# Layer 0's first five modulations as narrow fp32 products on TensorE, and four stages in a new written order

## The chip, the cores and the metric

One core of a Trainium2 chip runs the whole program once. The metric is device time in microseconds (us) of one launch. Instructions run on TensorE (PE in the profile, its weight loads PEld), VectorE (DVE), ScalarE (ACT), GpSimd (POOL) and SyncE (SP, which here only issues DMAs). Matrix products read from SBUF and write to PSUM, which has eight banks here called ps4 to ps7 and psl0 to psl3.

## The reference

One step of a four-layer backbone over 512 latent and 128 context tokens with 1024 features. In front of each half-layer stands a modulated norm, whose shift, scale and gate come from a linear map of a conditioning vector; there are two such vectors, `c` for latents and `c_ctx` for context tokens:

```python
def ada_mod(cond, w, b):
    m = jax.nn.silu(cond) @ w + b              # w: 1024 x 6144, one per layer
    return jnp.split(m[..., None, :], 6, axis=-1)

for i in range(DEPTH):                         # mixers A, B, C, A
    sh, sc, gt, sh2, sc2, gt2 = ada_mod(cond, w_ada[i], b_ada[i])   # for c and for c_ctx
    h = rmsnorm(x, norm_g[i, 0]) * (1 + sc) + sh
    x = x + gt * mixer(h)                      # attention, then its output projection
    h = rmsnorm(x, norm_g[i, 1]) * (1 + sc2) + sh2
    x = x + gt2 * (jnp.square(jax.nn.relu(h @ w_in)) @ w_out)
```

All is float32. The six parts are called modulation 0 (shift) to 5 (second gate) below.

## The kernel before

**Layout.** Activations lie with features on the 128 partitions (eight feature tiles, ft) and 640 tokens along the free axis, in two halves of 320. A product in float32 precision is made of three products of parts: each operand is split in a high part (ScalarE copies it to `fp32r`) and a low part (VectorE takes the difference), and high x high, high x low and low x high are added up in one bank. So one unit (128 output features) on one half is 24 products of 320 columns. In the trace the weights' parts are `wa`, the normed activations' `ex` and `ar`. Weights come as units of 512 KB through two `wraw` buffers on SyncE's queue.

**The modulations of layer 0 before the change.** A column of 128 outputs is a tile of 128 x 1024 of the transposed weights (512 KB). `ada_tile` loads it and takes a row-wise product with the conditioning vector that was copied to all partitions (`cb`): on VectorE as one multiply-and-reduce (`junk<-adaw,cb` or `junk<-wa,cb`), or, for the second vector of the tiles marked `mix`, as a multiply on GpSimd (`adaw<-adaw,cb`, `wa<-wa,cb`) and a summing pass on ScalarE. Layer 0 needs modulations 0 and 1 before anything else can start, 2 to 4 by its output projection and second norm. Four tiles of modulation 0 (`SPE`) are products on TensorE instead: the weights are the stationary operand, the two conditioning vectors a moving operand of two columns. `cb` itself is made on TensorE from a table (`sel`) in `start`.

**Stages of layer 0.** `start`: loads, modulations 0 and 1, the first half's norm (`norm_ft`: `nt<-x,mod,ps`, then `ex` or `ar` on ScalarE and `ar<-nt,...` on VectorE) and products of four ready units feature tile by feature tile as the norm goes on. `mixer_ac`, order "0 qkv": the second half's norm and products of the four units, and the values (five token blocks, 24 products of 256 columns each), with the tiles of modulations 2 and 3 as steps in between. Order "0 qkv2": two key units and four more query units, both halves, 12 x 24 products. "0 attn": attention. "0 oproj": eight units of the output projection, which also add to the residual and to the sum of squares (`acc`), the second norm, and the first eight units of the MLP; with the rest of modulations 3 and 4 as steps, modulation 5 and layer 1's behind them. On this stage `ws.slow` sends every second low part of the weights to GpSimd (`wa<-wraw,wa` on POOL).

**What sets the order.** In these five stages the calls are collected and replayed in an order written out by hand as a table of numbers (`ORDER`), which then is each engine's program order, in `start` SyncE's too. Outside them a scheduler orders. Each engine executes in order, so an instruction that waits holds all behind it.

Of the kernel before, what the change touches and what calls it, by code (L numbers as in the profile page):

```python
# [12 lines left out]
F32 = mybir.dt.float32  # L13
F32R = mybir.dt.float32r
# [4 lines left out]
P = 128  # L19
D = 1024  # L20
# [7 lines left out]
SPE = 4  # L28
SMIX = ((5, 7), (1, 3, 5, 7))
SX = {0: 5, 1: 6}  # L30
SJ = (0, 0, 2, 4, 5, 6)
# [3 lines left out]
A0S = 29  # L35
# [10 lines left out]
ORDER = {  # L46
    "0 attn": """
# [19 lines left out]
    """,  # L67
    "0 oproj": """
# [10 lines left out]
    """,  # L79
    "0 qkv": """  # L80
# [5 lines left out]
    """,  # L86
    "0 qkv2": """
# [4 lines left out]
    """,  # L92
    "0 start": """
# [710 lines left out]
class Kern:  # L804
# [289 lines left out]
    def mixer_ac(self, l):  # L1094
# [6 lines left out]
        with ExitStack() as lc:  # L1101
            if l == 0:
                aw = self.renew(self.walloc(3), F32)
                self.adaw = Ring(aw)
                steps = self.ada_tiles(0, range(16, A0S), True)
# [10 lines left out]
            with tc.tile_pool(name=f"qkv{l}", bufs=2) as tp:  # L1116
# [103 lines left out]
                if l == 0:  # L1220
                    values()
                    for _ in steps:
                        pass
                    oc.close()
                    self.wfree(self.renew(aw, F32R))
                    oc.enter_context(self.ordered(f"{l} qkv2"))
# [32 lines left out]
        def oproj():  # L1259
            step = None  # L1260
            if l == 0:
                steps = self.ada_tiles(0, range(A0S, 40), True)
                step = lambda: [next(steps, None) for _ in range(4)]
            self.run_units(8, [o[0] for o in O], [o[1] for o in O],
                           lambda ps, f, half: self.x_update(ps, f, half, m[2], True),
                           ret_last=lambda: self.norm_begin(l, 1), step=step)
            for o in O:
                self.free(o)
# [157 lines left out]
    def mlp(self, l, oproj):  # L1426

        nc = self.nc
        with self.tc.tile_pool(name=f"mlp{l}", bufs=1) as mp:
# [7 lines left out]
            self.ws.slow = (2, 6, 0, 0)[l]  # L1437
# [64 lines left out]
    def ada_tile(self, l, k, i, mix=False, dma=None):  # L1502

        nc = self.nc
        m = self.mods[l][k]
        w = self.adaw()
        (dma or (nc.sync if mix else nc.gpsimd)).dma_start(w, self.a["ada"][l, 8 * k + i])
        for cond in (0, 1):
            c = self.cb[:, cond, :]
            if cond and mix:  # L1510
                nc.gpsimd.tensor_tensor(out=w, in0=w, in1=c, op=ALU.mult)
                nc.scalar.activation(w, w, AF.Copy, accum_out=m[:, cond, i:i + 1])
            else:
                with self.tc.issue_after(self.last.ins) if self.last else nullcontext():
                    j = self.junk
                    nc.vector.tensor_tensor_reduce(out=j, in0=w, in1=c, op0=ALU.mult, op1=ALU.add, scale=1.0, scalar=0.0, accum_out=m[:, cond, i:i + 1])
        if i == 7 and (l or k > 1):
            self.mod_done(l, k)

    def ada_tiles(self, l, fs, mix=False):  # L1520
        for f in fs:
            self.ada_tile(l, f // 8, f % 8, mix)
            yield

    def silu(self, c, mp, n):
# [5 lines left out]
        nc.vector.tensor_tensor(out=c, in0=c, in1=e, op=ALU.mult)  # L1531

    def start(self):

        nc, a = self.nc, self.a
        with self.tc.tile_pool(name="start", bufs=6) as mp:
            self.adaw = self.ring(mp, "adaw", D, 6)
# [3 lines left out]
            wt = self.renew(self.alloc(12), F32)  # L1541
            oc = ExitStack()
            oc.enter_context(self.ordered("0 start", True))
            nc.sync.dma_start(c1, a["cc"])
            nc.sync.dma_start(c2, a["cc2"])
            for i in range(4):
                nc.sync.dma_start(wt[i][:16, :512], a["sel"][i // 2][:, i % 2 * 512:i % 2 * 512 + 512])
            self.silu(c1, mp, "e16")
            self.silu(c2, mp, "e8")
            own, self.banks = self.banks[:NQ[0]], self.banks[NQ[0]:]  # L1550
            for i in range(4):
                pb = self.bank()
                for j in range(4):
                    nc.tensor.matmul(pb[:, j * P:j * P + P], wt[i][:16, j * P:j * P + P], c1, start=True, stop=True)
                nc.scalar.activation(self.cb.rearrange("p c d -> p (c d)")[:, i * 512:i * 512 + 512], pb, AF.Copy)
            self.mods_open(0)
            m, b = self.mods[0], self.mods[0][6]
            ps = self.bank()
# [18 lines left out]
            for ft in range(NF):  # L1577
# [4 lines left out]
                if ft == 0:  # L1582
                    load_x(0, 0)
# [174 lines left out]
```

## Time and profile before

| | |
|---|---|
| median of 3 runs (lowest, highest) | 3115.05 us (3114.43, 3116.70) |
| the profiled execution, its own time | 3113.05 us |
| its span, first to last instruction | 3111.2 us |
| TensorE busy | 2981.5 us, 96% of the span, 20016 products |
| VectorE, ScalarE, GpSimd busy | 2232.6 (72%), 1373.2 (44%), 668.0 us (21%) |
| mean granted TensorE clock | 0.983 of full speed |

TensorE's share of nearly the whole span says that the kernel as a whole is bound by products; the stages before and after layer 0's attention are where it is not, and the profile is read there by stages. A busy TensorE need not run at its peak: the granted clock has two levels, 2.4 GHz (1.00) and 1.2 GHz (0.50), and a window's number is the mean over it.

### The profile page before, as it was taken

The page shows a single profiled execution, that of the slowest core. Times are in us where ns is not written, and L with a number is a line of the kernel's source. Part 1 is how long each engine was busy: PE and PEld are TensorE (multiplying, and loading weights), DVE is VectorE, ACT ScalarE, POOL GpSimd, SP SyncE. Part 2 cuts the span into 40 slices and gives each one's busy share as a digit, 9 for nine tenths or more (in the row PEclk, how much of TensorE's full clock was granted, in tenths as well). Part 3 has the DMA queues.
Part 4 walks back from the last instruction along what each step waited for, and adds up shares of the span by engine and source line. Part 5 has one row for each costly group of instructions (what it writes and reads, how often), then busy time and mean ns, then how long its engine had stood idle before and what let it go on. Part 6 is the DMA issues. An engine that isn't in the chain of part 4 may idle for free. (4 is left out here: it accounts for less than half of the span.)

```text
span 3111.2 us, 52045 instructions
## 1 busy us (share of the span) xinstructions
PE 2981.5 (96%) x20016; PEld 2916.1 (94%) x20016; DVE 2232.6 (72%) x4697; ACT 1373.2 (44%) x2895; POOL 668.0 (21%) x760
## 2 busy tenths in 40 slices
PE   6789899999999999999998899999999999999998
PEld 6789899999989989999998889999999899999998
DVE  8998987677679779667559997766756896633444
ACT  3477433223368664223237793332233494422321
POOL 4556420000034351000003571000000270000000
PEclk8799999999999999999999999999999999999999
DMA  6302444443212124444321004344422102222221
GB/s 220 107 25 75 142 155 145 150 153 126 65 39 58 50 87 146 150 149 149 97 80 35 23 1 151 121 151 150 148 85 75 45 1 69 95 75 75 75 75 48
DMA packets 89305, 300.84 MB, mean 97 GB/s; under 512 B 11104, under 2 KB 15920, under 8 KB 88672
## 3 DMA queue, kind: packets, MB, share of 16 engines
q1 hardware_dynamic: 64816, 210.35, 21.0%
q0 software_dynamic: 24240, 87.16, 8.8%
q8 instruction: 157, 2.57, 0.4%
q14 instruction: 92, 0.75, 0.1%
HBM read 288.66 MB, written 3.56 MB: 94 GB/s over the span
## 5 line engine op out<-in xcount | busy, mean ns | idle before, releaser
L283 PE MATMUL ps<-ar,wa 128*128 128x320 f32 x6752 | 1151.2, 312 | 22.5 <-DVE ar L283 15.3
L283 PE MATMUL psl<-ar,wa 128*128 128x320 f32 x6392 | 1088.8, 311 | 9.9 <-ACT ar L283 3.7
L283 PEld LDWEIGHTS ps<-ar,wa 128*128 128x128 f32 x6752 | 1038.2, 189 | 29.4 <-DVE ar L283 19.7
L283 PEld LDWEIGHTS psl<-ar,wa 128*128 128x128 f32 x6392 | 982.5, 189 | 12.9 <-ACT ar L283 4.1
L283 ACT ACTIVATE wa<-wraw 128x1024 fp32r<-128x1024 f32 (+3 forms) x350 | 359.9, 1030 | 938.4 <-PE psl L283 438.2
L283 DVE TENSOR_TENSOR wa<-wraw,wa 128x1024 fp32r<-128x1024 f32 (+2 forms) x336 | 410.6, 1222 | 280.3 <-ACT wa L283 279.4
L283 DVE CUSTOM_DVE_ANT_0 junk<-adaw,cb 128x1024 bf16<-128x1024 f32 x333 | 422.1, 1267 | 10.7 <-DMA adaw<-ada 10.1
L283 PE MATMUL ps<-ex,wa 128*128 128x320 f32 x1312 | 324.6, 316 | 15.1 <-ACT rpq L283 8.7
L283 PE MATMUL psl<-ex,wa 128*128 128x320 f32 x1312 | 322.1, 315 | 5.9 <-DVE wa L283 3.3
L283 POOL TENSOR_TENSOR p<-p,st 128x640 f32<-128x640 f32 (+2 forms) x256 | 277.3, 1106 | 174.6 <-DVE st L283 137.9
L283 POOL DMA_DIRECT2D adaw<-ada x152 | 81.1, 534 | 946.5 <-DVE mod L283 931.6
L283 PE MATMUL psl<-wa,ar 128*128 128x320 f32 (+3 forms) x1040 | 240.1, 335 | 20.9 <-DVE st L283 5.7
L283 PEld LDWEIGHTS ps<-ex,wa 128*128 128x128 f32 x1312 | 230.6, 192 | 19.2 <-ACT rpq L283 8.9
L283 DVE SCALAR_TENSOR_TENSOR x<-ps,mod,x 128x320 f32<-128x320 f32 (+2 forms) x264 | 107.3, 435 | 180.9 <-PE ps L283 180.8
L283 PEld LDWEIGHTS psl<-ex,wa 128*128 128x128 f32 x1312 | 228.8, 190 | 8.8 <-DVE wa L283 4.2
L283 DVE SCALAR_TENSOR_TENSOR x<-psl,mod,x 128x320 f32<-128x320 f32 (+2 forms) x240 | 98.4, 435 | 189.0 <-PE psl L283 189.0
L283 DVE TENSOR_TENSOR ar<-ps,ar 128x512 fp32r<-128x512 f32 (+3 forms) x416 | 223.0, 560 | 13.8 <-ACT ar L283 10.2
L283 ACT ACTIVATE ar<-ps 128x512 fp32r<-128x512 f32 (+5 forms) x452 | 208.0, 490 | 52.4 <-PE ps L283 48.6
L283 PEld LDWEIGHTS psl<-wa,ar 128*128 128x128 f32 x1040 | 169.5, 195 | 35.5 <-DVE st L283 14.5
L283 ACT ACTIVATE p<-p,st 128x640 f32<-128x640 f32 (+2 forms) x256 | 190.6, 748 | 19.2 <-DVE st L283 8.9
L283 PE MATMUL ps<-cst,p 128*128 128x128 f32 x1088 | 153.9, 273 | 4.7 <-DVE wa L283 2.7
L283 DVE TENSOR_TENSOR usq<-relu 128x320 f32<-128x320 f32 x256 | 128.4, 504 | 40.8 <-ACT relu L283 38.7
(206 smaller groups left out, 3049.5 us busy)
## 6 DMA issues: line engine op xcount, KB each, us to landing
adaw<-ada POOLq DMA_DIRECT2D x152, 512.0 KB, 4.6
wraw<-win SPq DMA_DIRECT2D x128, 512.0 KB, 3.4
wraw<-wout SPq DMA_DIRECT2D x128, 512.0 KB, 3.5
wraw<-qkv SPq DMA_DIRECT2D x36, 512.0 KB, 3.5
wraw<-wo SPq DMA_DIRECT2D x24, 512.0 KB, 3.5
adaw<-ada SPq DMA_DIRECT2D x23, 512.0 KB, 6.5
wa<-ada SPq DMA_DIRECT2D x13, 512.0 KB, 3.6
ar<-wa SPq DMA_DIRECT2D x64, 80.0 KB, 2.1
```

The lines of the kernel that those rows point to most:

```text
L283: return m(*a, **k)
```

## The change

Modulations 0 to 4 of layer 0 become products on TensorE in which the conditioning vectors are the stationary operand: `cs` holds eight blocks of 128 x 32, two columns of them filled, the rest zero. A tile of weights is now 128 of the 1024 inputs by 1024 outputs (`ada0`, `adan`, 512 KB), and `ada_pe` multiplies its four blocks of 256 columns, one product each, into the partitions 0, 32, 64 and 96 onward of one bank, summed over eight tiles. `ada_turn` copies the bank out on ScalarE and turns it with two transposes, `ada_put` adds bias and gain on VectorE for both vectors at once. Modulations 0 and 1 come in two parts, each with half the features of both, so that the first half of the norm's feature tiles can start after eight tiles. Tiles of modulations 2 to 4 are loaded on GpSimd's queue into four weight buffers and used in "0 qkv" only; no step is left in the output projection. GpSimd multiplies nothing for it, takes no low part of weights in this layer, and no longer adds the second half's squares in `start`. The bytes loaded are the same: 40 tiles of 512 KB, as before. The four tables "0 start", "0 qkv", "0 qkv2" and "0 oproj" are new; "0 attn" is unchanged.

```diff
-SPE = 4
-SMIX = ((5, 7), (1, 3, 5, 7))
-SX = {0: 5, 1: 6}
-SJ = (0, 0, 2, 4, 5, 6)
+PMODS = (2, 3, 4)
...
-A0S = 29
...
-                aw = self.renew(self.walloc(3), F32)
+                aw = self.renew(self.walloc(4), F32)
                 self.adaw = Ring(aw)
-                steps = self.ada_tiles(0, range(16, A0S), True)
+                steps = self.ada_steps(self.all_banks[-1])
+                self.banks = self.all_banks[:-1]
...
-            if l == 0:
-                steps = self.ada_tiles(0, range(A0S, 40), True)
-                step = lambda: [next(steps, None) for _ in range(4)]
...
-            self.ws.slow = (2, 6, 0, 0)[l]
+            self.ws.slow = (0, 6, 0, 0)[l]
...
+    def ada_pe(self, w, kt, ps):
+
+        for j in range(4):
+            self.nc.tensor.matmul(ps[32 * j:32 * j + 32, :256], self.cs[:, kt, :], w[:, 256 * j:256 * j + 256], start=kt == 0, stop=kt == 7)
+
+    def ada_turn(self, ps):
...
+        t = self.at()
+        nc.scalar.activation(t, ps[:, :256], AF.Copy)
+        nc.cut()
+        for i in (0, 1):
+            nc.tensor.transpose(ps[:, 256 + i * P:256 + i * P + P], t[:, i * P:i * P + P], self.ident)
...
+        for i, k in enumerate(PMODS):
+            for q in range(4):
+                ws = [self.adaw(), self.adaw()]
+                for j in (0, 1):
+                    nc.gpsimd.dma_start(ws[j], self.a["adan"][i, 2 * q + j])
+                nc.cut()
+                for j in (0, 1):
+                    self.ada_pe(ws[j], 2 * q + j, ps)
+                if q == 3:
+                    self.ada_put(k, self.ada_turn(ps), 0, 8)
+                yield
...
-                    self.sq_acc(xs(ft, half), half, ft == 0, eng=nc.gpsimd if half in (1,) else None)
...
+            for g in (0, 1):
                 for kt in range(8):
...
+                    self.ada_pe(w, kt, rest[g])
...
+                t = self.ada_turn(rest[g])
+                for k in (0, 1):
+                    self.ada_put(k, t[:, :, 2 * k:2 * k + 2], 4 * g, 4)
+                for ft in range(4 * g, 4 * g + 4):
+                    self.norm_ft(0, ft, m[0], m[1], r)
+                    for i, (w, p, kt) in enumerate(ready):
+                        nc.cut()
+                        self.mm_half(p, w, self.hh, self.hl, 0, kts=range(kt, ft + 1))
```

**TensorE, the start of the program.** `c` and `ar` are the old conditioning vectors and weight tiles, `ones<-acc` and `dg` belong to the norm, `adaw` are the loaded tiles and `cs` the new stationary operand. Before:

```order
L283 MATMUL ps_72<-c_156,ar_158 128x128 x4
L283 MATMUL ps_73<-c_156,ar_159 128x128 x4
L283 MATMUL ps_71<-c_156,ar_161 128x128 x4
L283 MATMUL ps_74<-c_156,ar_160 128x128 x4
L283 MATMUL ps_71<-ones,acc_65 128x1 x3
L283 MATMUL ps_72<-c_157,ar_162 128x2 x5
L283 MATMUL ps_72<-c_157,ar_163 128x2 x3
L283 MATMUL ps_72<-c_157,ar_164 128x2 x5
L283 MATMUL ps_72<-c_157,ar_165 128x2 x3
L283 MATMUL ps_73<-dg_146,cst 128x128 x2
```

Now, in the same place:

```order
L276 MATMUL ps_71<-adaw_0_152,cs 32x256 x4
L276 MATMUL ps_71<-adaw_1_153,cs 32x256 x4
L276 MATMUL ps_71<-adaw_2_154,cs 32x256 x4
L276 MATMUL ps_71<-adaw_3_155,cs 32x256 x4
L276 MATMUL ps_72<-adaw_0_152,cs 32x256 x4
L276 MATMUL ps_71<-adaw_4_156,cs 32x256 x4
L276 MATMUL ps_71<-adaw_5_157,cs 32x256 x4
L276 MATMUL ps_74<-ones,acc_65 128x1 x3
L276 MATMUL ps_71<-adaw_6_158,cs 32x256 x4
L276 MATMUL ps_71<-adaw_7_159,cs 32x256 x4
L276 MATMUL ps_71<-cst,at_0_135 128x128 x2
```

The products that spread the vector to all partitions and those of two columns are gone; groups of four products of 32 x 256 stand there, one group for each loaded tile, eight groups before the first transposes. One group of part two (into ps_72) stands ahead of the last four of part one.

**VectorE, the second half's norm in "0 qkv".** `nt` and `ar` are the norm, `rps` and `rpq` the rotary step of finished units, `ISA junk` a multiply-and-reduce of a modulation tile. Before:

```order
L283 SCALAR_TENSOR_TENSOR ar_92<-nt_0_142,mod_0_173,ar_84 128x192
L283 TENSOR_TENSOR rpq_1_567<-psl_1_79,tab_0_559 128x320
L283 SCALAR_TENSOR_TENSOR nt_1_143<-x,mod_0_174,ps_74 128x128
L283 ISA junk,mod_0_175<-wa_541,cb_134 128x1024
L283 ISA mod_0_175 128x1
L283 TENSOR_TENSOR rpq_0_566<-psl_2_80,tab_0_559 128x320
L283 SCALAR_TENSOR_TENSOR ar_92<-nt_1_143,mod_0_173,ar_84 128x128
```

Now:

```order
L276 TENSOR_TENSOR rpq_1_507<-psl_1_79,tab_0_499 128x320
L276 SCALAR_TENSOR_TENSOR ar_91<-nt_0_144,mod_0_164,ar_83 128x192
L276 SCALAR_TENSOR_TENSOR nt_0_144<-x,mod_0_165,ps_71 128x192
L276 STREAM_SHUFFLE rps_0_504<-psl_2_80 128x320
L276 SCALAR_TENSOR_TENSOR ar_92<-nt_0_144,mod_0_164,ar_84 128x192
L276 SCALAR_TENSOR_TENSOR ar_92<-nt_1_145,mod_0_164,ar_84 128x128
```

The norm and the rotary step follow each other with no modulation tile between them.

**GpSimd, the same stage.** `rps<-rps,tab` is its part of the rotary step, `wa` here are the buffers with modulation tiles. Before:

```order
L283 TENSOR_TENSOR wa_541<-wa_541,cb_134 128x1024
L283 TENSOR_SCALAR sink_553<-sink_553 128x16
L283 TENSOR_TENSOR rps_0_564<-rps_0_564,tab_1_560 128x320
L283 TENSOR_TENSOR wa_542<-wa_542,cb_134 128x1024
L283 TENSOR_TENSOR wa_543<-wa_543,cb_134 128x1024
L283 TENSOR_TENSOR rps_1_565<-rps_1_565,tab_1_560 128x320
```

Now:

```order
L276 TENSOR_TENSOR rps_0_504<-rps_0_504,tab_1_500 128x320
L276 TENSOR_TENSOR rps_1_505<-rps_1_505,tab_1_500 128x320
L276 DMA wa_480<-adan 128x1024
L276 DMA wa_481<-adan 128x1024
L276 DMA wa_482<-adan 128x1024
L276 DMA ck_0_503<-cv 128x256
L276 TENSOR_TENSOR rps_0_504<-rps_0_504,tab_1_500 128x320
```

The multiplies are gone, and the loads that SyncE issued stand here instead, between the rotary steps; the first four of the 24 loads stand at the head of GpSimd's program.

## Rows read from the trace of the kernel before

**Rows 1.** Windows: busy us (x instructions) of each engine, granted clock, DMA share, GB/s.
```profile
0.00:4.00 4.00, 0.00 (x0) 0.00 (x0) 0.35 (x4) 1.59 (x2) 1.98 (x7) 1.00 0.35 86
4.00:32.60 28.60, 20.91 (x92) 20.11 (x93) 24.66 (x51) 10.07 (x21) 6.20 (x3) 1.00 1.01 369
32.60:71.00 38.40, 28.20 (x126) 26.20 (x126) 35.72 (x68) 14.99 (x30) 22.05 (x17) 0.82 0.39 140
71.00:107.30 36.30, 23.90 (x98) 20.06 (x97) 35.94 (x58) 16.70 (x34) 19.91 (x12) 0.67 0.36 109
107.30:126.40 19.10, 16.07 (x121) 15.66 (x120) 18.46 (x29) 8.03 (x18) 13.54 (x8) 0.91 0.39 121
126.40:135.00 8.60, 0.00 (x0) 0.00 (x0) 8.34 (x10) 3.23 (x6) 5.31 (x4) 0.64 0.57 179
135.00:187.80 52.80, 46.35 (x288) 45.57 (x289) 49.03 (x108) 28.37 (x67) 17.94 (x19) 0.93 0.18 61
...
290.00:440.00 150.00, 132.66 (x859) 130.03 (x859) 130.97 (x213) 63.50 (x122) 65.07 (x33) 0.94 0.48 161
```

**Rows 2.** What TensorE waited for, 0 to 440 us: us, times, longest.
```profile
PE ps L283 <- DVE ar L283: 12.0, 7, 2.6
PE ps L283 <- ACT rpq L283: 8.7, 1, 8.7
PE ps L283 <- DVE acc L283: 8.4, 1, 8.4
```

**Rows 3.** VectorE groups by form, 0 to 440 us: busy, mean ns, idle before.
```profile
L283 DVE CUSTOM_DVE_ANT_0 junk<-adaw,cb 128x1024 bf16<-128x1024 f32 x46 | 70.0, 1521 | 5.0 <-DMA adaw<-ada 4.7
...
L283 DVE CUSTOM_DVE_ANT_0 junk<-wa,cb 128x1024 bf16<-128x1024 f32 x13 | 17.6, 1354 | 0.1
```

**Rows 4.** GpSimd groups by form, 0 to 440 us.
```profile
L283 POOL TENSOR_TENSOR adaw<-adaw,cb 128x1024 f32<-128x1024 f32 x17 | 47.8, 2825 | 43.3 <-DVE mod L283 29.0 <-DVE rs L283 14.4
L283 POOL TENSOR_TENSOR wa<-wa,cb 128x1024 f32<-128x1024 f32 x13 | 33.8, 2603 | 24.9 <-DVE mod L283 24.9
...
L283 POOL TENSOR_TENSOR wa<-wraw,wa 128x1024 fp32r<-128x1024 f32 x10 | 26.7, 2673 | 46.6 <-ACT wa L283 44.6 <-issue 1.8
```

**Rows 5.** VectorE in order of time: start, us, operation.
```profile
13.85 1.22 DVE L283 CUSTOM_DVE_ANT_0 junk<-adaw,cb 128x1024 bf16<-128x1024 f32 x1
...
58.84 3.38 DVE L283 CUSTOM_DVE_ANT_0 junk<-adaw,cb 128x1024 bf16<-128x1024 f32 x1
```

**Rows 6.** GpSimd in order of time, same stretch.
```profile
58.54 2.61 POOL L283 TENSOR_TENSOR adaw<-adaw,cb 128x1024 f32<-128x1024 f32 x1 [1.17 <-DVE mod L283]
```

**Rows 7.** DMA issues of the page: KB each, us to landing.
```profile
adaw<-ada POOLq DMA_DIRECT2D x152, 512.0 KB, 4.6
```

**Rows 8.** TensorE in order of time: start, us, operation, xcount.
```profile
7.58 7.34 PE L283 MATMUL ps<-c,ar 16*128 16x128 f32 x32 [7.58 <-DMA ar<-sel]
...
120.49 0.40 PE L283 MATMUL ps<-wa,ex 128*128 128x256 f32 x2
...
123.35 0.40 PE L283 MATMUL psl<-wa,ex 128*128 128x256 f32 x2
...
293.45 3.68 PE L283 MATMUL psl<-ar,wa 128*128 128x320 f32 x24
296.97 3.68 PE L283 MATMUL ps<-ar,wa 128*128 128x320 f32 x24
```

**Rows 9.** A TensorE group of the page: xcount, busy us, mean ns.
```profile
L283 PE MATMUL ps<-ar,wa 128*128 128x320 f32 x6752 | 1151.2, 312 | 22.5 <-DVE ar L283 15.3
```

**Rows 10.** VectorE groups by form, 0 to 440 us: the norm's operations.
```profile
L283 DVE SCALAR_TENSOR_TENSOR nt<-x,mod,ps 128x320 f32<-128x320 f32 x16 | 8.2, 540 | 0.4 <-PE ps L283 0.2
...
L283 DVE SCALAR_TENSOR_TENSOR nt<-x,mod,ps 128x192 f32<-128x192 f32 x16 | 6.4, 407 | 0.1
...
L283 DVE SCALAR_TENSOR_TENSOR nt<-x,mod,ps 128x128 f32<-128x128 f32 x16 | 5.4, 341 | 1.0 <-PE ps L283 0.8
...
L283 DVE SCALAR_TENSOR_TENSOR ar<-nt,mod,ex 128x320 fp32r<-128x320 f32 x8 | 4.2, 541 | 0.0
```

More of the change, by code (lines that the diff above doesn't have):

```diff
@@ L46 @@
 ORDER = {
+    "0 oproj": """
[9 rows of a table added]
+    """,
+    "0 qkv2": """
[4 rows of a table added]
+    """,
+    "0 qkv": """
[5 rows of a table added]
+    """,
+    "0 start": """
[4 rows of a table added]
+    """,
     "0 attn": """
@@ L66 @@
         691 693 698 699 694 706 702 701 695 709 704 710 703 712 714 708 707 705 711 717 718 713 716 719 721 722 715 720 723 724 725
-    """,
-    "0 oproj": """
[10 rows of a table removed]
-    """,
-    "0 qkv": """
[5 rows of a table removed]
-    """,
-    "0 qkv2": """
[4 rows of a table removed]
-    """,
-    "0 start": """
[6 rows of a table removed]
     """,
@@ L1225, in mixer_ac @@
                     self.wfree(self.renew(aw, F32R))
+                    self.banks = self.all_banks
                     oc.enter_context(self.ordered(f"{l} qkv2"))
@@ L1259, in oproj @@
         def oproj():
[L1260 to L1263 removed]
             self.run_units(8, [o[0] for o in O], [o[1] for o in O],
                            lambda ps, f, half: self.x_update(ps, f, half, m[2], True),
[L1266 removed]
+                           ret_last=lambda: self.norm_begin(l, 1))
             for o in O:
@@ L1500, in cb_load, with ada_tile @@
         e.dma_start(self.cb, self.sil.rearrange("c d -> (c d)").partition_broadcast(P).rearrange("p (c d) -> p c d", c=2))
-    def ada_tile(self, l, k, i, mix=False, dma=None):
+    def ada_tile(self, l, k, i):
         nc = self.nc
@@ L1506, in ada_tile, with ada_tiles, silu @@
         w = self.adaw()
-        (dma or (nc.sync if mix else nc.gpsimd)).dma_start(w, self.a["ada"][l, 8 * k + i])
+        nc.gpsimd.dma_start(w, self.a["ada"][l, 8 * k + i])
         for cond in (0, 1):
[L1509 to L1517, printed above, removed]
+            with self.tc.issue_after(self.last.ins) if self.last else nullcontext():
+                nc.vector.tensor_tensor_reduce(out=self.junk, in0=w, in1=self.cb[:, cond, :], op0=ALU.mult, op1=ALU.add, scale=1.0, scalar=0.0, accum_out=m[:, cond, i:i + 1])
+        if i == 7:
             self.mod_done(l, k)
-    def ada_tiles(self, l, fs, mix=False):
+    def ada_tiles(self, l, fs):
         for f in fs:
-            self.ada_tile(l, f // 8, f % 8, mix)
+            self.ada_tile(l, f // 8, f % 8)
             yield
-    def silu(self, c, mp, n):
+    def silu(self, c, mp, n, out):
         nc = self.nc
@@ L1530, in silu, with ada_put, ada_steps @@
         nc.vector.reciprocal(e, e)
-        nc.vector.tensor_tensor(out=c, in0=c, in1=e, op=ALU.mult)
+        nc.vector.tensor_tensor(out=out, in0=c, in1=e, op=ALU.mult)
+    def ada_pe(self, w, kt, ps):
+        for j in range(4):
+            self.nc.tensor.matmul(ps[32 * j:32 * j + 32, :256], self.cs[:, kt, :], w[:, 256 * j:256 * j + 256], start=kt == 0, stop=kt == 7)
+    def ada_turn(self, ps):
+        nc = self.nc
+        t = self.at()
[3 more added lines that the diff above has]
+            nc.tensor.transpose(ps[:, 256 + i * P:256 + i * P + P], t[:, i * P:i * P + P], self.ident)
+        return ps[:, 256:].rearrange("p (i j q) -> p q j i", i=2, q=32)[:, 0:2]
+    def ada_put(self, k, t, f0, n):
+        nc = self.nc
+        b, o = self.mods[0][6], self.mods[0][k][:, :, f0:f0 + n]
+        r = lambda c: b[:, c + f0:c + f0 + n].rearrange("p (c f) -> p c f", c=1).to_broadcast([P, 2, n])
+        r4 = lambda c: r(c).rearrange("p c (j i) -> p c j i", i=2)
+        nc.vector.tensor_tensor(out=o.rearrange("p c (j i) -> p c j i", i=2), in0=t, in1=r4(8 * k), op=ALU.add)
+        if k in (1, 4):
+            nc.vector.scalar_tensor_tensor(out=o, in0=o, scalar=1.0, in1=r(48 + (k - 1) // 3 * 8), op0=ALU.add, op1=ALU.mult)
+    def ada_steps(self, ps):
+        nc = self.nc
+        for i, k in enumerate(PMODS):
[9 more added lines that the diff above has]
+                yield
     def start(self):
@@ L1536, in start @@
         with self.tc.tile_pool(name="start", bufs=6) as mp:
-            self.adaw = self.ring(mp, "adaw", D, 6)
+            aw = self.ring(mp, "adaw", D, 8)
             c1 = mp.tile([16, P], F32, name="c16", bufs=1)
@@ L1540, in start @@
             self.hh, self.hl = self.ex + self.alloc(4), self.alloc(8)
-            wt = self.renew(self.alloc(12), F32)
             oc = ExitStack()
             oc.enter_context(self.ordered("0 start", True))
-            nc.sync.dma_start(c1, a["cc"])
             nc.sync.dma_start(c2, a["cc2"])
[L1546 to L1555, printed above, removed]
+            nc.vector.memset(self.cs, 0.0)
+            self.silu(c2, mp, "e8", self.cs[:, :, 0:2])
+            own, rest = self.all_banks[:NQ[0]], self.all_banks[NQ[0]:]
             self.mods_open(0)
-            m, b = self.mods[0], self.mods[0][6]
-            ps = self.bank()
-            self.banks = [p for p in self.banks if p is not ps]
+            m = self.mods[0]
             xs = lambda ft, half: self.x[:, ft, half * HT:half * HT + HT]
@@ L1564, in load_x @@
                 for ft in range(f, f + 4):
-                    self.sq_acc(xs(ft, half), half, ft == 0, eng=nc.gpsimd if half in (1,) else None)
-            def on_pe(i):
-                w = wt[4 + 2 * (i % 4):6 + 2 * (i % 4)]
-                nc.sync.dma_start(w[0], a["ada0"][i][:, :T])
-                nc.sync.dma_start(w[1][:, :D - T], a["ada0"][i][:, T:])
-                for kt in range(8):
-                    nc.tensor.matmul(ps[:, 2 * i:2 * i + 2], w[kt // 5][:, kt % 5 * P:kt % 5 * P + P], c2[:, kt, :], start=kt == 0, stop=kt == 7)
@@ L1574, in start @@
-            self.ws.cap = 0
-            self.ws.slow = 0
-            ready = []
-            for ft in range(NF):
-                if ft < SPE:
-                    on_pe(ft)
-                else:
-                    self.ada_tile(0, 0, ft, ft in SMIX[0], nc.sync)
-                if ft == 0:
-                    load_x(0, 0)
-                self.ada_tile(0, 1, ft, ft in SMIX[1], nc.sync)
-                if ft == 0:
-                    load_x(0, 4)
-                    r = self.rstd(0, D)
-                    self.banks = [p for p in self.banks if p is not r]
-                for h in SX:
-                    if ft == SX[h]:
-                        load_x(1, 4 * h)
-                c = slice(ft, ft + 1)
-                nc.vector.tensor_tensor(out=m[0][:, 0, c], in0=ps[:, 2 * ft:2 * ft + 1] if ft < SPE else m[0][:, 0, c], in1=b[:, c], op=ALU.add)
-                nc.vector.tensor_tensor(out=m[1][:, 0, c], in0=m[1][:, 0, c], in1=b[:, 8 + ft:9 + ft], op=ALU.add)
-                nc.vector.scalar_tensor_tensor(out=m[1][:, 0, c], in0=m[1][:, 0, c], scalar=1.0, in1=b[:, 48 + ft:49 + ft], op0=ALU.add, op1=ALU.mult)
-                self.norm_ft(0, ft, m[0], m[1], r)
-                while self.ws.cap < NQ[0] and ft >= SJ[self.ws.cap]:
-                    self.ws.cap += 1
-                    ready.append((self.ws.get(), own[self.ws.cap - 1], 0))
-                for i, (w, p, kt) in enumerate(ready):
-                    self.mm_half(p, w, self.hh, self.hl, 0, kts=range(kt, ft + 1))
-                    ready[i] = (w, p, ft + 1)
@@ new lines, in load_x @@
+                    self.sq_acc(xs(ft, half), half, ft == 0)
+            self.ws.cap = self.ws.slow = 0
+            load_x(0, 0)
+            load_x(0, 4)
+            self.banks = rest[2:]
+            r = self.rstd(0, D)
+            ready = []
+            for g in (0, 1):
+                for kt in range(8):
+                    w = aw()
+                    nc.sync.dma_start(w, a["ada0"][g, kt])
+                    nc.cut()
+                    self.ada_pe(w, kt, rest[g])
+                self.ws.cap += 2
+                for i in (2 * g, 2 * g + 1):
+                    ready.append((self.ws.get(), own[i], 0))
+                t = self.ada_turn(rest[g])
[4 more added lines that the diff above has]
+                    for i, (w, p, kt) in enumerate(ready):
+                        nc.cut()
+                        self.mm_half(p, w, self.hh, self.hl, 0, kts=range(kt, ft + 1))
+                        ready[i] = (w, p, ft + 1)
@@ L1603, in start @@
             self.ready = ready
-            nc.vector.tensor_tensor(out=m[0][:, 1, :SPE], in0=ps[:, :2 * SPE].rearrange("p (f c) -> p c f", c=2)[:, 1, :], in1=b[:, :SPE], op=ALU.add)
-            nc.vector.tensor_tensor(out=m[0][:, 1, SPE:], in0=m[0][:, 1, SPE:], in1=b[:, SPE:8], op=ALU.add)
-            nc.vector.tensor_tensor(out=m[1][:, 1, :], in0=m[1][:, 1, :], in1=b[:, 8:16], op=ALU.add)
-            nc.vector.scalar_tensor_tensor(out=m[1][:, 1, :], in0=m[1][:, 1, :], scalar=1.0, in1=b[:, 48:56], op0=ALU.add, op1=ALU.mult)
+            load_x(1, 0)
@@ L1608, in start @@
+            load_x(1, 4)
+            self.banks = [p for p in rest if p is not r][:2]
             self.r1 = self.rstd(1, D)
+            nc.sync.dma_start(c1, a["cc"])
+            self.silu(c1, mp, "e16", c1)
             self.banks = self.all_banks
@@ L1611, in start @@
             oc.close()
-            self.free(self.renew(wt, F32R))
             nc.gpsimd.dma_start(self.gf, a["gf"])
@@ L1646, in main @@
         self.a0 = self.a0_cm.enter_context(self.tc.tile_pool(name="ada0", bufs=1, side="right"))
-        self.cb = self.a0.tile([P, 2, D], F32, name="cb0")
+        self.cs = self.a0.tile([P, 8, 32], F32, name="cs")
+        self.at = self.ring(self.a0, "at", 256, 2)
         self.open_x()
@@ L1676, in layout @@
     o["cc2"] = c(np.stack([inp["c"].reshape(8, P), inp["c_ctx"].reshape(8, P)], 2).transpose(1, 0, 2))
-    o["ada0"] = c(inp["w_ada"][0, :, :D].reshape(8, P, 8, P).transpose(2, 1, 0, 3).reshape(8, P, D))
+    o["ada0"] = c(inp["w_ada"][0, :, :2 * D].reshape(8, P, 2, 2, 512).transpose(3, 0, 1, 2, 4).reshape(2, 8, P, D))
+    o["adan"] = c(inp["w_ada"][0, :, 2 * D:5 * D].reshape(8, P, len(PMODS), D).transpose(2, 0, 1, 3))
     o["ada"] = c(inp["w_ada"].reshape(DEPTH, D, 48, P).transpose(0, 2, 3, 1))
@@ L1682, in layout @@
     o["cst"] = c(np.stack([np.full((P, P), -0.5), np.eye(P), np.kron(np.eye(2), np.ones((64, 64)))], 1).astype(np.float32))
-    o["sel"] = c(np.kron(np.eye(16), np.ones((1, P))).reshape(16, 2, D).transpose(1, 0, 2).astype(np.float32))
     o["rope"] = rope_tables(64, 32, 2)
```

47 rows, old and new, of the table ORDER are left out of this document.

## The prediction, made before the changed kernel ran

> **What bounds the kernel now.** The page's first part gives TensorE 96% of the span, so I first looked for the places where TensorE is not busy, in the table of windows [rows 1]. The reader is to see two things there: how far TensorE's busy time falls short of a window's length, and which engine comes nearest to filling the window instead. From 32.6 to 71.0 us (first half's norm) TensorE has 28.2 of 38.4 us and VectorE 35.7; from 71.0 to 107.3 (second half) 23.9 against 35.9 of 36.3; from 107.3 to 126.4 (values) 16.1 against 18.5 of 19.1; then 8.6 us without any product; from 135.0 to 187.8 (keys, queries) 46.4 against 49.0 of 52.8. Until attention begins, VectorE is all but full. The granted clock (0.82, 0.67, 0.91, 0.64) says more: in windows where TensorE had stood still, part of its work then ran at the lower level of 1.2 GHz, so its busy time there is stretched too. Output projection and first MLP units, 290 to 440 us: 132.7 of 150 at 0.94.
>
> The list of TensorE's waits [rows 2] names the releasers: normed activations from VectorE, 12.0 us in seven waits; one wait of 8.7 for `rpq`; one of 8.4 for `acc`, the sum of squares in the output projection. `rpq` is ScalarE's, but it stands behind the modulations' summing passes there.
>
> Why VectorE is full is in its groups [rows 3]: 46 + 13 = 59 multiply-reduces, 87.6 us, mean 1.485. GpSimd's groups [rows 4] show 30 multiplies (81.6 us) and ten low parts (26.7). In order of time the two collide: a multiply-reduce took 1.22 us while GpSimd was idle and 3.38 while it multiplied [rows 5, 6]. So GpSimd's work lengthens VectorE's.
>
> **What goes.** Of the 59, the 42 that belong to modulations 0 to 4 (18 in the start, 13 in "0 qkv", 11 in the output projection): 42 x 1.485 = 62 us of VectorE. All 30 multiplies of GpSimd and ScalarE's 30 summing passes behind them. The ten low parts move to VectorE: at 1.22, the duration of the undisturbed operation on a tile of the same 128 x 1024 [rows 5], 12 us come back in the output projection. The old fp32 products in the start go too; they lay under the loads, so I count nothing for them.
>
> **What comes: the price of a group.** TensorE gets 40 groups of four products of 256 columns, 16 in the start and 24 in "0 qkv". An fp32 product of 128 columns took 7.34 / 32 = 0.229 us [rows 8], so one of 256 columns takes 0.458. Bounds: if the four run at once, as each fills only 32 columns of the array and its own partitions, a group costs 0.46 us; one after another, 1.83. For each of 34 changes between narrow and full products I add the 165 ns by which a product's 312 ns [rows 9] exceeds the pitch of a stream, 3.52 / 24 = 147 ns [rows 8], as if the overlap were lost there: 34 x 0.165 / 40 = 0.14. No row of before has narrow products side by side; between the ends I take the low one, because neither array columns nor partitions are shared: 0.6 us per group.
>
> The Trainium skill, TensorE: Matmul & The Clock Gate, Part 3 (packing small matmuls), says that products in different column groups run at the same time, with 2.38 times the rate for three; scaled to four (an estimate, 3.2) that makes 1.83 / 3.2 = 0.58 per group, and the sum as below. No run here shows it. The Trainium skill, TensorEngine Tiling (Array Packing), Key Properties, speaks against the change: to alter the tiling mode empties TensorE. It gives no price, and no row of before has such a switch; if it cost nothing, the sum would be 5.6 us less.
>
> **The start.** Loads set its first part: 369 GB/s from 4.0 to 32.6, after 0.34 MB [rows 1]. The last tile of part one lands behind 9.37 MB (8 tiles and 7 other loads of 512 KB [rows 7], the first half's x in two of 0.655, 0.2 of small ones): 4 + 9.03 / 0.369 = 28.5 us. A group, ScalarE's copy, two transposes and the first norm put the first wide product near 32, as before (32.6): no gain yet. Part two needs nine more loads, 4.72 MB: 41.3 us; the second half's x, 1.31 MB, lands at 44.8 and hinders nothing earlier. From 41.3: a group 0.6, the turn about 2, then on VectorE four feature tiles at 2 x 0.54 [rows 10], seven additions of squares at about the same and 1 for the modulations, 9 together, then the last 12 products at 0.147, 1.8. Half 0 is done at 54.7, say 55, where it now ends at 71.0.
>
> **"0 qkv" and "0 qkv2".** Second half: four units x 3.52 = 14.1 [rows 8], 14 groups x 0.6 = 8.4. VectorE's norm is 8 x (0.41 + 0.34) x 2 = 12 us [rows 10] and lies mostly beside them; I leave 4 for TensorE's waits on it. 55 + 26.5 = 81.5. Values: five blocks x 2.86 [rows 8] and 10 x 0.6 = 20.3, to 102. The 8.7 us wait goes with the passes that caused it. Keys and queries: 12 x 3.52 = 42.2 and 4 of waits, to 148; attention's first product 2.5 later, at 150.5, where it now comes at 187.8: 37 us. The tables are new, and each engine runs in order; I hold back 3 us for stalls: 34.
>
> **Output projection.** TensorE's idle time is 150 - 132.7 = 17.3 [rows 1], half of it the one wait of 8.4 for `acc`; the clock takes at most 0.06 x 132.7 = 8. VectorE loses 11 x 1.485 = 16 us there, and modulation 5's tiles no longer stand among its work, which also runs undisturbed by GpSimd; it gains the 12 above. I keep about 7 of the 25 as waits that stay: gain 18. Behind 440 us everything is bound by products, and a shift arrives at the end unchanged.
>
> **Sum.** 34 + 18 = 52 from 3113.05, the profiled execution's own time: 3061. The median lies 2 above that execution: **3063 us**.
>
> **Rivals.**
>
> A. The above, 3063; its own range 3050 to 3080. Chance 0.60.
>
> B. The four products run one after another: 1.23 us more per group. "0 qkv": 24 x 1.23 = 29.5, some 4 of it inside waits. Start: part one's groups can begin when its first tile lands, behind 5.57 MB, at 18.2; nine groups x 1.83 reach 34.7, not 29.1, and part two's then end some 9 us later. Together 35: 3098. For it: they share one stationary operand and one stream of instructions. Against it: separate columns and partitions. 0.17.
>
> C, the other side: one after another *and* at the lower clock in the start. TensorE waits for loads between groups there, and after such waits the clock of before fell (0.82 from 32.6 on [rows 1]). A group is then 3.66 us; 16 groups x 1.83 more is 29, of which some 4 lie inside the waits for tiles: 3098 + 25 = 3123. It decides from a mean of about 2.3 us per group on, where the 52 are used up. 0.06.
>
> D. VectorE is relieved, but TensorE is held by the new orders: a load that stands behind a waiting one on SyncE or GpSimd. SyncE's load of part two's first tile waits for a buffer that TensorE must free, and two tiles of part one stand behind it; TensorE takes part two's first group before the last of part one; "0 qkv" has four buffers in turn, 4.6 us from issue to landing [rows 7]. Half of the gain, 26: 3087. 0.12.
>
> E. No change: what VectorE gives back in these stages, TensorE spends on groups and turns; 3113 to 3118, centre 3115. The old list of waits speaks against it, as its largest are all VectorE's or ScalarE's. 0.05.
>
> **The numbers.** Low end: without the changes' 5.6 us, without the 3 held back, with 5 more in the output projection and 3 more in "0 qkv": 3046. High end: B's 3098 and 3 us. Outside are C, E, and the tails of A, B and D, somewhat under 0.2. A measurement of this kernel tells about 0.2% (6 us) from no change: A, B and D are faster (0.89, less 0.02 for their tails), E mostly the same, C slower.
>
> **What would show it.** Groups of four at a pitch near 0.5 to 0.6 us and with starts almost together (right), or 0.46 apart (B), or 0.9 apart (C). First wide product near 32 us; half 0 done near 55; attention's first product near 150. No multiply on GpSimd, VectorE's operations of one form with nearly one duration. From 55 to 150 TensorE busy above 85% and a clock above 0.9. The wait of 8.4 for `acc` gone. It would be wrong if TensorE's waits in the start are for loads that come later than 28.5 and 41.3 us (D), if VectorE still fills the windows from 55 to 150 us, or if TensorE is busy there with groups at more than 2 us.

## The result and the profile after

The changed kernel takes 3068.37 us (median of 4 runs, 3067.67 to 3070.04) against 3114.74 before: 46.4 us less, a ratio of 0.9851 with a 95% interval of 0.9834 to 0.9869. 3063 was forecast, with a range of 3046 to 3101. The two profiled executions stand 42.9 us apart by their spans (3111.2 and 3068.3): the one of before lies 1.7 us below its median, the one of the changed kernel 1.7 above. All places below are read from them.

The windows of the changed kernel over the stretches of [rows 1] (busy us and instructions of TensorE, its weight loads, VectorE, ScalarE, GpSimd; granted clock, DMA share, GB/s):

```profile
4.00:32.60 28.60, 10.11 (x78) 3.96 (x78) 7.02 (x18) 5.92 (x14) 1.13 (x3) 1.00 1.03 395
32.60:71.00 38.40, 33.64 (x226) 23.72 (x227) 30.62 (x84) 17.81 (x40) 8.26 (x14) 0.92 0.52 181
71.00:107.30 36.30, 35.60 (x329) 29.69 (x329) 17.59 (x43) 12.87 (x29) 14.19 (x25) 0.99 0.83 298
107.30:135.00 27.70, 27.41 (x205) 25.83 (x204) 18.76 (x46) 12.45 (x31) 6.09 (x8) 1.00 0.28 86
135.00:187.80 52.80, 45.68 (x280) 41.83 (x279) 49.46 (x142) 35.16 (x96) 25.55 (x44) 0.94 0.08 23
...
290.00:440.00 150.00, 149.17 (x1019) 148.52 (x1019) 108.08 (x221) 52.48 (x98) 5.27 (x10) 1.00 0.37 120
```

From 71 to 135 us, where TensorE had 40.0 of 64.0 us, it now has 63.0, and VectorE 36.3 where it had 62.7. The clock is near 1.00 there. (The same stretch of time now holds later work, as every stage begins earlier.) The list of what TensorE waits for, 0 to 440 us (total us, times, longest):

```profile
PE ps L276 <- DMA adaw<-ada: 22.4, 4, 19.2
PE ps L276 <- DVE wa L276: 7.4, 3, 3.7
PE psl L276 <- DVE rpq L276: 2.5, 1, 2.5
PE ps L276 <- ACT ex L276: 1.8, 2, 1.5
PE ps L276 <- DVE ar L276: 1.0, 2, 0.7
```

The waits of 8.7 and 8.4 and most of the 12.0 for `ar` of [rows 2] are gone; in front stand the loads of the first tiles. TensorE in order of time (start, us, operation, records):

```profile
22.19 2.79 PE L276 MATMUL ps<-adaw,cs 128*32 128x256 f32 x24 [1.93 <-DMA adaw<-ada]
...
30.55 1.93 PE L276 MATMUL ps<-adaw,cs 128*32 128x256 f32 x16
...
38.73 0.41 PE L276 MATMUL psl<-ex,wa 128*128 128x320 f32 x1 [0.32 <-ACT ex L276]
...
43.53 0.64 PE L276 MATMUL ps<-adaw,cs 128*32 128x256 f32 x8
...
54.21 5.08 PE L276 MATMUL psl<-ar,wa 128*128 128x320 f32 x33
...
59.12 0.31 PE L276 MATMUL ps<-ex,wa 128*128 128x320 f32 x1
...
81.87 1.93 PE L276 MATMUL ps<-wa,cs 128*32 128x256 f32 x32
83.73 0.41 PE L276 MATMUL psl<-ex,wa 128*128 128x320 f32 x1
...
159.73 2.53 PE L276 MATMUL psl<-wa,ar 128*128 128x384 f32 x8 [2.52 <-DVE rpq L276]
...
262.57 3.68 PE L276 MATMUL ps<-ar,wa 128*128 128x320 f32 x24
...
396.82 14.24 PE L276 MATMUL psl<-ar,wa 128*128 128x320 f32 x96
```

Each group of four fp32 products leaves eight records, two for each product (so the "20016 products" of the table of before are records, too). The x32 at 81.87 are four groups in 1.86 us, 0.465 each; the x24 at 22.19 three groups at 0.93. The first full product comes at 38.7 us (32 was forecast), half 0 is done at 59.1 (55), attention begins at 159.7 (150.5; 187.8 before), 28.1 us earlier. The other 14.8 of the 42.9 come behind that. The last two lines are the first product of the output projection and a block of the MLP. The same two in the kernel before:

```profile
289.93 3.68 PE L283 MATMUL ps<-ar,wa 128*128 128x320 f32 x24
...
440.93 14.24 PE L283 MATMUL psl<-ar,wa 128*128 128x320 f32 x96
```

The lead is 27.4 us at the first and 44.1 at the second, so 16.7 were won in between (18 forecast), where the wait of 8.4 for `acc` is gone. Attention lost 0.7 of the lead, and what follows lost 1.2 to the end.

### The profile page after: what moved, and what is told of

The parts are those of the page before. It is cut to its first block, busy times and chain, and to the rows that moved or that the text cites. A ratio compares the mean times of both kernels' runs of the same rounds, so it can differ in the third digit from the quotient of the medians.

```text
span 3068.3 us, 52252 instructions
## 1 busy us (share of the span) xinstructions
PE 2968.7 (97%) x20250; PEld 2889.8 (94%) x20250; DVE 2121.1 (69%) x4605; ACT 1339.6 (44%) x2836; POOL 561.2 (18%) x737
## 5 line engine op out<-in xcount | busy, mean ns | idle before, releaser
L276 DVE TENSOR_TENSOR wa<-wraw,wa 128x1024 fp32r<-128x1024 f32 (+3 forms) x346 | 417.2, 1206 | 291.0 <-ACT wa L276 290.0
L276 DVE CUSTOM_DVE_ANT_0 junk<-adaw,cb 128x1024 bf16<-128x1024 f32 x304 | 372.6, 1226 | 10.6 <-DMA adaw<-ada 10.0
L276 PE MATMUL ps<-ex,wa 128*128 128x320 f32 x1304 | 317.9, 312 | 6.0 <-DVE wa L276 3.7
L276 DVE SCALAR_TENSOR_TENSOR x<-psl,mod,x 128x192 f32<-128x192 f32 (+2 forms) x240 | 98.4, 436 | 186.2 <-PE psl L276 186.2
L276 ACT ACTIVATE p<-p,st 128x640 f32<-128x640 f32 (+2 forms) x256 | 190.6, 748 | 20.2 <-DVE st L276 9.3
```

What stands on the lines that cost most here:

```text
L276: return m(*a, **k)
```

## Experiments

Every time below is a median beside runs of the kernel before on the same chip (3114.40 to 3114.67). "The changed kernel" is the 3068.37 of above unless another is named.

**Twice the groups, side by side or in one strip of columns.** The zero columns of `cs` make extra products that add nothing; the second kernel has `ps[:30, :256]` for the output.

```diff
-                    self.ada_pe(ws[j], 2 * q + j, ps)
+                    if q + j == 0:
+                        self.ada_pe(ws[j], 0, ps)
+                    for p in range(4):
+                        nc.tensor.matmul(ps[32 * p:32 * p + 30, :256], self.cs[:, 0, 2:], ws[j][:, 256 * p:256 * p + 256], start=False, stop=False)
+                    if q + j:
+                        self.ada_pe(ws[j], 2 * q + j, ps)
```

> In the second half's stage ("0 qkv") each of the 24 groups is done twice; the second four products have a stationary operand of zeros and add nothing. Theory N (the four products of a group run side by side, 0.465 us a group at full pace): 24 x 0.465 = 11 us more, less up to 3 that fall into waits, so 8 to 11 us above the changed kernel. Rival S (one after another, 1.83 us): 44 us more, less some 4.

> As the kernel with the 24 groups done twice, but the four extra products of a group all go to partitions 0 to 29, so to the same columns of the array. Theory N (they run side by side only because each has columns of its own): 4 x 0.465 = 1.86 us an extra group, 24 x 1.86 = 45 us above the changed kernel, less some 4. Rival S (columns do not matter): the same time as with the groups done twice.

Measured: 3076.40 us (ratio 0.988, 0.9865 to 0.9895) and 3104.89 us (0.997, 0.9959 to 0.9981), so 8.0 and 36.5 us above the changed kernel. TensorE, first of the one, then of the other:

```profile
66.29 1.93 PE L276 MATMUL ps<-wa,cs 128*30 128x256 f32 x32
```

```profile
72.11 4.50 PE L276 MATMUL ps<-wa,cs 128*30 128x256 f32 x32
```

The two lines have the same number of products, two real groups and two extra ones. Taking two real groups as 0.93 us, the two extra ones cost about 0.93 in four strips and 3.5 in one, 3.8 times as much (the prediction's estimate from three strips was 3.2). Side by side is shown (theory N), with 36.5 us for the one strip where 41 was expected. A strip of columns is also a strip of partitions of the bank; the two weren't tried apart. Had the 24 real groups stood in one strip as well, some 28 us of the gain would be gone (an estimate: 36.5 less 8.0), close to what rival B took for them (29.5, less 4 in waits). B's mechanism isn't what happens.

**Thin groups.** Leaves out most of modulations 2 to 4.

```diff
-                    self.ada_pe(ws[j], 2 * q + j, ps)
+                    n = 256 if q + j == 0 else 16
+                    for p in range(4):
+                        nc.tensor.matmul(ps[32 * p:32 * p + 32, :n], self.cs[:, 2 * q + j, :], ws[j][:, 256 * p:256 * p + n], start=q + j == 0, stop=2 * q + j == 7)
```

> Leaves out most of modulations 2 to 4: in "0 qkv" 21 of the 24 groups multiply 16 columns instead of 256; loads, turns and order stay. If the groups stand on the path, as the sum had it: 21 x 0.4 = 8 us less than the changed kernel. Rival (they lie in waits for the second half's norm, and cost nothing): within 2 us of it.

Measured: 3063.34 us (0.984, 0.9824 to 0.9857), 5.0 below the changed kernel, between the 8 and the 2 expected. The groups lie on the path for the most part, not wholly. What TensorE waits for in this kernel from 55 to 110 us shows what takes their place:

```profile
PE ps L276 <- DMA wa<-adan: 4.2, 4, 2.1
```

In the changed kernel that wait is 0.7 us: where groups are short, the next tile isn't there yet.

**Low parts back on GpSimd, in the changed kernel; off GpSimd, in the one before.**

```diff
-            self.ws.slow = (0, 6, 0, 0)[l]
+            self.ws.slow = (2, 6, 0, 0)[l]
```

In the kernel before the same line changes the other way.

> The changed kernel, but every second low part of layer 0's output projection and MLP weights goes back to GpSimd (2.67 us each instead of 1.22). Theory M (the gain in the output projection came from the multiply-reduces that left VectorE): within 3 us of the changed kernel. Rival (GpSimd's low parts were what held TensorE there): 6 to 12 us slower.

> The kernel before, with only the ten low parts of the output projection and MLP weights moved from GpSimd to VectorE (12 us more on VectorE at 1.22). Theory M (VectorE was full there with multiply-reduces): 0 to 6 us slower than before. Rival (GpSimd's low parts were what held TensorE): 4 to 10 us faster.

Measured: 3071.03 us (0.9863, 0.9849 to 0.9878), 2.7 above the changed kernel, and 3116.63 (1.0008, 0.9999 to 1.0017), no change that can be told. These ten low parts are a small matter in either kernel; the rivals fall. The 12 us more on VectorE didn't come, though: without the low parts on GpSimd its busy time in the whole execution fell from 2232.6 to 2227.0 us, with ten operations more. GpSimd's low parts had stretched VectorE's operations beside them. A form of the MLP shows it (0 to 440 us; before, then in the changed kernel, which has no low parts on GpSimd either):

```profile
L283 DVE TENSOR_TENSOR ar<-usq,ar 128x320 fp32r<-128x320 f32 x16 | 12.4, 788 | 0.5
```

```profile
L276 DVE TENSOR_TENSOR ar<-usq,ar 128x320 fp32r<-128x320 f32 x16 | 7.6, 486 | 4.5 <-ACT ar L276 4.4
```

In the kernel before with its low parts on VectorE the mean is 488 ns, in the changed kernel with them on GpSimd 622; there VectorE's busy time stayed, 2121.1 and then 2121.3 us, though it had ten operations fewer.

**The kernel before without GpSimd's multiplies.** Three kernels: the first gives their products to VectorE, the second leaves out most of each multiply, the third most of each summing pass on ScalarE (both leave out most of the second vector's part of the mixed tiles).

```diff
-                nc.gpsimd.tensor_tensor(out=w, in0=w, in1=c, op=ALU.mult)
-                nc.scalar.activation(w, w, AF.Copy, accum_out=m[:, cond, i:i + 1])
+                nc.vector.tensor_tensor_reduce(out=self.junk, in0=w, in1=c, op0=ALU.mult, op1=ALU.add, scale=1.0, scalar=0.0, accum_out=m[:, cond, i:i + 1])
+                nc.scalar.activation(self.junk[:, :8], self.junk[:, :8], AF.Copy)
```

```diff
-                nc.gpsimd.tensor_tensor(out=w, in0=w, in1=c, op=ALU.mult)
+                nc.gpsimd.tensor_tensor(out=w[:, :16], in0=w[:, :16], in1=c[:, :16], op=ALU.mult)
```

```diff
-                nc.scalar.activation(w, w, AF.Copy, accum_out=m[:, cond, i:i + 1])
+                nc.scalar.activation(w[:, :8], w[:, :8], AF.Copy, accum_out=m[:, cond, i:i + 1])
```

> The kernel before, with GpSimd's 30 multiplies as multiply-reduces on VectorE instead; ScalarE's summing pass becomes one of 8 columns. Theory M (VectorE's amount of work sets the stages up to attention): 30 x 1.22 = 37 us more on VectorE, less the 59 x 0.26 = 16 that the collisions cost: some 15 to 25 us slower than before. Rival (the collisions with GpSimd were the main cost): within 5 us of before, or faster.

> The kernel before, with GpSimd's 30 multiplies over 16 of 1024 columns; this leaves out most of the second vector's products of the mixed tiles, while loads, ScalarE's passes and VectorE's instructions stay. Theory C (GpSimd's long multiplies are the cost: they stretch VectorE's instructions beside them and hold what waits for them): VectorE's multiply-reduces fall from 1.49 to about 1.25 us, and the time by 28 to 40 us, more than the 20 of the kernel that gave VectorE those products. Rival M (only the amount of work on VectorE counts, which is the same here): within 8 us of before.

> The kernel before, with ScalarE's 30 summing passes over 8 of 1024 columns; this leaves out most of the second vector's sums of the mixed tiles, while GpSimd's multiplies stay whole. Theory C (the multiplies cost by their length and what they do to VectorE): 0 to 8 us faster than before. Rival P (ScalarE's passes hold the norm and the rotary step behind them, as in the wait of 8.7 us for rpq): 12 to 25 us faster.

Measured: 3094.38 us (0.9936, 0.9922 to 0.995), 20.2 *faster* than before though VectorE does 30 products more, so theory M falls as I had it; 3057.98 (0.982, 0.9805 to 0.9835), 56.7 faster, theory C's direction and more than its 28 to 40; 3116.17 (1.0002, 0.9992 to 1.0011), nothing. It is the multiplies, not the passes. VectorE's groups by form, 0 to 440 us (busy, mean ns): before, then with the multiplies cut short.

```profile
L283 DVE SCALAR_TENSOR_TENSOR ar<-rpq,ar 64x320 fp32r<-64x320 f32 x32 | 22.8, 720 | 0.8
L283 DVE TENSOR_TENSOR acc<-acc,sq 128x320 f32<-128x320 f32 x21 | 18.5, 890 | 4.2 <-ACT sq L283 3.7
L283 DVE TENSOR_TENSOR rpq<-rpq,rps 128x320 f32<-128x320 f32 x10 | 9.2, 919 | 1.5 <-POOL rps L283 1.1
```

```profile
L283 DVE CUSTOM_DVE_ANT_0 junk<-adaw,cb 128x1024 bf16<-128x1024 f32 x61 | 75.3, 1235 | 4.5 <-DMA adaw<-ada 4.0
L283 DVE SCALAR_TENSOR_TENSOR ar<-rpq,ar 64x320 fp32r<-64x320 f32 x32 | 16.6, 526 | 0.8
L283 DVE CUSTOM_DVE_ANT_0 junk<-wa,cb 128x1024 bf16<-128x1024 f32 x13 | 16.2, 1250 | 0.1
L283 DVE TENSOR_TENSOR acc<-acc,sq 128x320 f32<-128x320 f32 x21 | 11.4, 551 | 3.6 <-ACT sq L283 3.0
L283 DVE SCALAR_TENSOR_TENSOR nt<-x,mod,ps 128x320 f32<-128x320 f32 x16 | 8.2, 541 | 0.7 <-PE ps L283 0.6
L283 DVE TENSOR_TENSOR rpq<-rpq,rps 128x320 f32<-128x320 f32 x10 | 4.9, 489 | 1.5 <-POOL rps L283 1.1
```

Not only the multiply-reduces of [rows 3] were stretched, but other forms, too. Those whose means fell read two operands from SBUF; `nt<-x,mod,ps`, which has one of its two in PSUM, kept the 540 ns of [rows 10] (how many of these met a multiply the list doesn't tell). Taking each form's count before times the fall of its mean, over all forms, gives 56.7 us, of which the multiply-reduces are 46 x 0.286 + 13 x 0.104 = 14.5. The time fell by 56.7. And 56.7 less 30 products of 1.25 us is 19, where 20.2 was measured. VectorE's busy time in the whole execution agrees: 2232.6 us before, 22.8 less in the first kernel and 56.2 less in the second. In these stages of the kernel before, a microsecond of VectorE is thus about a microsecond of the whole. That doesn't hold without end: the low parts' 5.6 us above brought nothing that can be told, and the changed kernel has 111.5 less for 46.4 of time. (That the stretch alone is the cause rests on this agreement: GpSimd's queue is freed by the same edits, and its part wasn't tried apart.) One place of the kernel before shows the mechanism, VectorE and then GpSimd in order of time:

```profile
62.47 2.21 DVE L283 SCALAR_TENSOR_TENSOR mod<-mod,adab 128x1 f32<-128x1 f32 x1
```

```profile
62.32 2.34 POOL L283 TENSOR_TENSOR adaw<-adaw,cb 128x1024 f32<-128x1024 f32 x1 [1.17 <-DVE rs L283]
```

An operation on one column took 2.21 us, until GpSimd's multiply had ended (62.32 + 2.34 = 64.66; VectorE 64.68). The Trainium skill, SBUF — State Buffer, section "SBUF: two separate sides", has the rule: VectorE with two inputs from SBUF and GpSimd share a pair of ports, which the one that starts first holds for a whole instruction while the other stands still. The two rows agree with it.

**TensorE's pace in the start.**

```diff
+                    for _ in range(40 * (g == 0 and kt == 0)):
+                        nc.tensor.matmul(rest[g][:, 256:384], self.ident, self.mh, start=True, stop=True)
                     self.ada_pe(w, kt, rest[g])
+                    for _ in range(3 * (8 * g + kt in (0, 1, 2, 3, 8))):
+                        nc.tensor.matmul(rest[g][:, 256:384], self.ident, self.mh, start=False, stop=False)
```

The first kernel has the loop of 40 alone, the second both; then the changed kernel and the second once more, on one chip.

> The changed kernel with 40 fp32 products of 128 x 128 on a constant table put ahead of TensorE's first group, into a bank that is written anew after. Theory P (the first full product comes at 38.7 us, not at 32, because TensorE works at half pace in the start: 0.93 us a group, slow transposes): groups at about 0.47 us, first full product at 34 to 35.5, the first half done 3 to 4 us earlier, 2 to 4 us less in all. Rival L (the loads set it): first full product at 38 to 39, time within 1 us.

> As the kernel with 40 products ahead of the first group, and three more such products behind each of the first five groups, which fill part of TensorE's waits for the next tile. Theory P with a pace that falls again in those waits: here the groups go on at 0.47 us and the first full product comes at 34 to 35, while with the 40 alone the pace is lost again. If it does not fall in waits of 2 us: no difference to the 40 alone but for up to 1 us. Rival L: 38 to 39 us, or later by the added work.

> The changed kernel once more, unaltered, on the same chip as the one with extra products in the start. Theory P (TensorE's pace in the start differs between executions and moves the first full product, between 34.7 and 38.7 us, by itself): median 3067 to 3070.

> The kernel with 40 products ahead of the first group and three behind each of the first five, once more. If the pace in the start is worth time in the end: 1 to 3 us less than the changed kernel on the same chip. Rival (what is won in the start is lost again in waits before attention): within 1 us.

Measured: 3068.58 us (0.9856, 0.9842 to 0.9869), 3067.06 (0.9849, 0.9836 to 0.9863), 3067.43 (0.9851, 0.9835 to 0.9867), 3068.52 (0.9851, 0.9837 to 0.9866). All four are one time within what can be told, and the 3068.37 of above with them; on the one chip the extra products cost 1.1 us and didn't bring 1 to 3. The traces do show the pace. With the 40 alone TensorE stands still for 4.46 us behind them, and its groups then run at 0.93 us, so this kernel didn't try what it was meant to; its windows:

```profile
4.00:19.00 15.00, 10.54 (x86) 10.13 (x85) 0.20 (x2) 0.00 (x0) 1.15 (x3) 0.94 1.02 388
19.00:32.60 13.60, 9.34 (x78) 3.73 (x70) 6.41 (x16) 5.87 (x13) 0.00 (x0) 0.50 1.03 404
```

The clock there is at its lower level, 1.2 GHz. With the waits filled, groups go over to 0.465 at about 25 us in one run and 27 in the other, and the first full product comes at 36.8 and 37.8, against 38.7 and 39.4 in the changed kernel's two: earlier, but not the 34 to 35 expected. The plainest case came by itself, in the run with the low parts on GpSimd, whose start is the changed kernel's word for word:

```profile
27.05 1.07 PE L276 MATMUL ps<-adaw,cs 128*32 128x256 f32 x16 [0.63 <-DMA adaw<-ada]
...
34.75 0.41 PE L276 MATMUL psl<-ex,wa 128*128 128x320 f32 x1 [0.23 <-ACT ex L276]
```

Two groups in 0.93 us, and the first full product at 34.8, 4.0 us earlier. Half 0 is done 3.0 us earlier (56.1) and the values begin 3.2 earlier (86.2); in the values TensorE then waits 1.2 us for a tile on GpSimd's queue, and attention keeps 1.7 (157.99 against 159.73). With the waits filled attention begins at 159.5 and 159.7, in the changed kernel at 159.7 and 160.7, so at most 1 us is kept, and the medians show none. So theory P holds for the place, and not for the time.

The new order tables and the squares that left GpSimd weren't tried apart from the rest of the change.

## Why the prediction came out right, step by step

- **The sum.** 46.4 us measured, 52 forecast. By the traces 28.1 up to attention (34 forecast), 16.7 in the output projection and the first MLP units (18), and 1.9 lost in attention and behind. Attention began 9.2 us later than the 150.5 of the sum, of which 3 were held back. The mechanism held: VectorE is no longer the bound, and TensorE runs through. In the stretch from 55 to 150 us that the prediction named (busy above 85%, clock above 0.9) TensorE is busy for 87.7 of 95 us, 92%, at a mean clock of 0.96, and VectorE for 64.0:

```profile
55.00:80.00 25.00, 22.22 (x156) 16.36 (x155) 19.58 (x56) 10.68 (x26) 8.39 (x13) 0.86 0.44 154
80.00:100.00 20.00, 19.30 (x187) 15.65 (x186) 9.10 (x25) 6.68 (x14) 8.04 (x14) 1.00 0.82 296
100.00:150.00 50.00, 46.22 (x347) 43.39 (x345) 35.27 (x82) 23.00 (x54) 12.21 (x16) 1.00 0.31 103
```

- **The price of a group**, 0.6 us: in the stream 0.465, with the switches 1.00 us for two and a little more on the next block, so about 0.54; in the start 0.93. The value was about right, the reading behind it wrong: I took the x32 of [rows 8] for 32 products. The program has 16 there, each fp32 product leaves two records, and a product of 128 columns took 0.459 us, at half pace. Twice too many products and half the pace cancelled, which was luck.
- **The start** was mis-sized by 4.1 us (59.1 for 55). The loads came as forecast or a little earlier (395 GB/s for 369). But nine groups, the sums for the norm and the transposes ran at half pace: part one's last group ended at 32.5 instead of 29.1, and part two's last group began at 43.5 instead of 41.3. In the run with the low parts on GpSimd, at full pace from 25.8 us, that group waited for its load and began at 40.4, so the pace cost 3.1 us there. Behind it the turn was 0.9 us shorter than summed and VectorE's 9 us came as forecast, but TensorE then had 33 products left (the line at 54.21) where the sum had 12: 4.8 us for 1.8, in either run. So pace and order of work cost about 3 us each, and loads and turn gave back 0.9 each. Part of C's condition was thus met, the low level in the start; with the groups side by side it cost 3.0 us at the end of half 0 (59.1 against 56.1), and 1.7 at attention.
- **"0 qkv" up to the values** took 30.2 us from 59.1 to 89.4, for 26.5 forecast. Groups (8.3 us for 8.4) and waits (3.5 for 4) were right. The 96 wide products took 18.1 us for 14.1: by the rows of this stretch 2.3 of the 4 went to eleven products at the low clock between 65.9 and 72.0 us (granted clock 0.51 from 65 to 72, within the 0.86 of the first line above), and 1.1 to twelve that stand singly between waits at its head. The sum had all of them at full pace, without a gap.
- **The values**, with their groups, took 20.1 (20.3 forecast); keys and queries 50.3 up to attention (48.5), with waits of 2.0 and 1.7 for low parts of weights and of 2.5 for `rpq`, where VectorE is nearly full again (30.4 of 33.0 us from 127 to 160).
- **What VectorE is relieved of** I had under-counted: 62 us of multiply-reduces, with the collisions only in their own mean. The collisions reach its other operations, too, 56.7 us in all, 42 of them outside the multiply-reduces; and the ten low parts that I charged with 12 us cost VectorE nothing net. That this did no harm is because the sum was built on what TensorE has to do once VectorE is out of the way.
- **Rivals.** B and C lack their premise, products one after another; D showed up as single waits, not as half of the gain; E did not occur.

## What to carry to other kernels

Work that is moved to GpSimd to relieve VectorE has to be charged with what it does to VectorE's other instructions: compare the means of short forms inside and outside such a stretch, not of the moved form alone. Here giving the products back to a nearly full VectorE was worth 20 us, against 46 for the whole change, in which TensorE takes them and the orders are new. Before a record count is turned into a price, it has to be held against the number of instructions in the program.

## What was not expected of the hardware

The granted clock of the first stretches reads 1.00 (4.0 to 32.6 us above) while groups took 0.93 us, twice their later 0.465; the same pace behind the 40 products reads 0.50. In the first stretch the pitch of like products tells the pace, and the clock's row does not. And the same start ran at full pace from about 25.8 us in the run with the low parts on GpSimd, and at half pace up to some 37 us in the changed kernel's; what decides it no run here told.
